# A hybrid decoder trunk on one NeuronCore: half of the modulation rows multiplied on GpSimd and summed by ScalarE, with three tiles for them and four for raw weights

## The chip, the cores and the metric

The kernel runs on one NeuronCore of a Trainium2 chip. The metric is the device time of one execution in microseconds (us). TensorE (PE) multiplies matrices; VectorE (DVE), ScalarE (ACT) and GpSimd (POOL) work element by element; SyncE (SP) issues nearly all transfers from device memory. Each engine works through its own queue in order and waits for others by semaphores.

## The reference, cut to what matters

A trunk of two layers over 256 tokens of 2048 features in float32. Each of its four sub-layers (mixer and FFN of layer 0, mixer and FFN of layer 1) is modulated by shift, scale and gate, which come from one vector `c`:

```python
def ada_modulation(c, w, b):
    mod = (jax.nn.silu(c) @ w + b)[:, None, :]
    shift, scale, gate = jnp.split(mod, 3, axis=-1)
    return shift, scale, gate

def swiglu(h, w1, w3, w2):
    return (jax.nn.silu(h @ w1) * (h @ w3)) @ w2

    for i in range(DEPTH):
        shift, scale, gate = ada_modulation(c, ada_mix_w[i], ada_mix_b[i])
        h = rms_norm(x) * (1.0 + scale) + shift
        ...
        x = x + gate * y
        shift, scale, gate = ada_modulation(c, ada_ffn_w[i], ada_ffn_b[i])
        h = rms_norm(x) * (1.0 + scale) + shift
        x = x + gate * swiglu(h, ffn_w1[i], ffn_w3[i], ffn_w2[i])
    return rms_norm(x) * final_norm_w
```

Each `w` of the modulation is 2048 x 6144, so four of them are 201 MB of the 706 MB that the kernel moves. As `c` is one row, this product is not made on TensorE. The mixer of layer 0 runs RWKV-7 and a gated delta rule side by side, that of layer 1 is Mamba-2.

## The kernel before

**Matrix products.** Activations lie transposed, features on partitions and 256 tokens along the row. A float32 product is made of three TensorE products in a rounded format: weights and activations are split in a high and a low part (`whi`, `wlo`; `hhi`, `hlo`, and so on), and high x high, high x low and low x high are summed in PSUM (`products`, L749). Weights stream in through `raw` tiles of up to 128 x 1024 (512 KB; RAW = 5, L89). ScalarE rounds a tile to `whi`, VectorE subtracts to get `wlo` (`split_next` L659, `low_parts` L703), then the `raw` tile is free for the next load. Of `whi` and `wlo` there are three each (PARTS, L92), so that `whi` is made about two pieces ahead of its use.

**Slabs.** The first product of a sub-layer runs as a slab (`lin_slab`, L775): 16 rows, one for each 128 features of the normalised input, and in each row several output tiles, so that TensorE can start on feature block 0 while later blocks are still being normalised. In a row VectorE multiplies `t` by the norm, ScalarE adds the shift and rounds to `hhi`, VectorE subtracts to `hlo` (`norm_mod`, L840, `shifted`). The shift of row kt has to be known by then (`modc`, L650). In the first slab of all, that of layer 0's mixer, the norm's multiply (`xin`) and `hlo` run on GpSimd (`first`, L1913).

**Modulation rows.** 128 outputs of a modulation are one row (l, r, n): sub-layer l, r = 0 for shift, 1 for scale, 2 for gate, block n of 16. The shift and scale of the first sub-layer are made from 1 MB tiles (`ini`) in the first slab. The other 160 rows are halved, 128 x 1024 each (512 KB), and loaded into `adat` tiles (ADAS = 2). For each of the 320 halves VectorE multiplies by the broadcast silu(c) (`silc`) and sums in one instruction (`ada_half`, L620; CUSTOM_DVE_ANT_0 in the trace, ISA in the program, followed by a read of the accumulator, DVE_READ_ACCUMULATOR2_ANT). The second half starts from the first's sum, so they go in order; the first starts from the bias. A scale gets 1.0 added.

**What sets the order.** The Python code writes the instructions of all engines in one sequence and holds each engine to it. A clock with estimated costs (`Clock.cost`, L301) runs along. Main thread is TensorE's stream of products; after each step the code lets chains of the mixers go on, makes pieces ahead, and calls `fill_ada` (L633). That places a half on VectorE when by the clock VectorE is 500 ns behind TensorE, or at most 2000 ns ahead if the half is due. Halves queue in `adaq`, spread over the weights of the stages ahead by `plan` (L551), and may be loaded up to 48 weight tiles early (`issue_ada`, L612). Where `modc` needs a row that isn't known yet, it takes halves at once, wherever that stands in VectorE's order. All loads, of `raw` and of `adat`, go through SyncE's queue in the order in which they were written; one that waits for its tile holds those behind it.

Of the kernel before, what the change touches and what calls it, by code (L numbers as in the profile page):

```python
# [10 lines left out]
F32 = mybir.dt.float32  # L11
# [7 lines left out]
P = 128  # L19
# [66 lines left out]
LAG = 4  # L86
SOON = 1000.0
INI = 6
RAW = 5  # L89
PIECE = 8  # L90
LEAD = 2
PARTS = 3  # L92
WORK0 = 6
WORK1 = 10
IDLE = 500.0
ADAS = 2
FILL = -500.0
LATE = 2000.0
DUE = 1.0
# [154 lines left out]
class Clock:  # L254
# [46 lines left out]
    def cost(self, i, name):  # L301
        e = i.engine
        o = i.outs[0]
        n = max(self.n(x) for x in list(i.outs) + list(i.ins) if getattr(x, "ap", None))
        t = mybir.EngineType
        if e == t.PE:
            nn, m = self.n(o), self.n(i.ins[1])
            if name == "transpose":
                return 109.0
            if i.ins[0].dtype == F32R:  # L310
                return max(107.0, 0.425 * nn)
            if m <= 64:
                return max(50.0 if m <= 32 else 81.0, 1.05 * nn)
            return max(430.0 if nn < 60 else 214.0, 1.68 * nn)
        if e == t.DVE:
            ps = any(getattr(getattr(x, "bass_ap", None), "tensor", None) is not None
                     and x.bass_ap.tensor.name.startswith("bank") for x in list(i.outs) + list(i.ins))
            if name in ("tensor_scalar", "tensor_copy") and not ps:
                return 65.0 + 0.53 * n
            return (130.0 if name == "scalar_tensor_tensor" else 70.0) + 1.05 * n  # L320
        if e == t.Activation:
            return 95.0 + 0.83 * n
        if e == t.Pool:
            return 500.0 if n <= 16 else 120.0 + (4.0 if name == "tensor_scalar" else 2.4) * n
        return 60.0

# [69 lines left out]
def trunk(ctx: ExitStack, tc: tile.TileContext, I, out):  # L396
# [180 lines left out]
    ifree = list(range(INI))  # L577
    st = {"raw": 0, "item": 0, "off": 0, "hold": True}
    lows = []
    raws, parts, known, sums = {}, [], set(), {}  # L580
    after_ada = {}
    adat = [wp.tile([P, 1024], F32, name=f"adat{q}") for q in range(ADAS)]
    aname = [name_of(t) for t in adat]
    adas = []

    def load_ada(t, l, r, n, e):
        SP.dma_start(t, I["ada"][l, 16 * r + n, e])
# [22 lines left out]
        issue_raw()  # L610

    def issue_ada():  # L612
        while adaq and len(adas) < ADAS and adaq[0][4] <= st["item"] + EARLY:
            q = next(q for q in range(ADAS) if q not in [a[0] for a in adas])
            if adas and clock.since(aname[q]) > clock.at(ET.PE) + QUEUE:
                return
            adas.append((q,) + adaq.pop(0))
            load_ada(adat[q], *adas[-1][1:5])

    def ada_half(t, l, r, n, e):  # L620

        if e == 0:
            sums[l, r, n] = cp.tile([P, 1], F32, tag="adap", name=nm("adap"), bufs=6)
        pt = sums[l, r, n]
        o = mod[:, l, 16 * r + n:16 * r + n + 1] if e else pt
        V.tensor_tensor_reduce(t, t, silc[:, 1024 * e:1024 * (e + 1)], 1.0,
                               pt if e else prc("adab", 48 * l + 16 * r + n), ALU.mult, ALU.add, o)
        if e:
            if r == 1:
                V.tensor_scalar(o, o, 1.0, None, ALU.add)  # L630
            known.add((l, r, n))

    def fill_ada(until=None):  # L633

        issue_ada()
        while adas:
            q, l, r, n, e, due = adas[0]
            v = clock.at(ET.DVE)
            if until is None:
                until = clock.at(ET.PE) + (LATE if due <= st["item"] else FILL)  # L640
# [4 lines left out]
    def take_ada():  # L645
        q = adas.pop(0)
        ada_half(adat[q[0]], *q[1:5])
        issue_ada()

    def modc(l, r, n):  # L650
        while (l, r, n) not in known:
            if not adas:
                q = adaq[0][:4] + (0,)
                adaq[0] = q
                issue_ada()
            take_ada()
        return mod[:, l, 16 * r + n:16 * r + n + 1]

    def split_next(rows=None):  # L659
# [1320 lines left out]
```

## Time and profile before

| | us |
|---|---|
| median of 3 runs | 3011.66 (3009.58 to 3016.07) |
| the profiled execution's own time | 3014.75 |
| its span, first to last instruction | 3012.9 |
| mean granted TensorE clock | 0.981 |
| waits of VectorE for loads of `adat` | 30.7, in 33 places |

The stages in the profiled execution, in us from the span's start: 30 to 145 the first slab, 145 to 740 the rest of layer 0's mixer and its output product, 744 to 812 the slab of layer 0's FFN, to 1500 the rest of that FFN, 1560 to 2080 the Mamba mixer after its slab, 2290 to 3012 the FFN of layer 1 after its slab. A row of a group gives, after the operands and the count, the busy time in us, the mean of one in ns, the idle time of the engine before it in us, and what ended that idle time. In a timeline the first two numbers are the start and the duration in us; in brackets stands the idle time before it and what ended it. All instructions are recorded by one helper, so that the line (L372) tells nothing and the tiles' names tell all.

### The profile page before, as it was taken

How to read it: one execution, taken by the hardware profiler on the slowest of the kernel's cores; microseconds unless marked ns; L12 is line 12 of the kernel's file. 1: busy time of each engine (PE TensorE's matmuls, PEld its weight loads, DVE VectorE, ACT ScalarE, POOL GpSimd, SP SyncE). 2: the span in 40 equal slices, each digit the busy share in tenths (PEclk: the TensorE clock that was granted, in tenths of full speed). 3: DMA queues.
4: the chain of work that ended last, by engine and by line, in shares of the span. 5: the costliest groups of instructions: out<-in, count | busy, mean ns of one | idle time of the engine just before them, and what ended most of it. 6: DMA issues, size and time to landing. Idle time of an engine off the chain costs nothing.

```text
span 3012.9 us, 61369 instructions
## 1 busy us (share of the span) xinstructions
PE 2884.7 (96%) x25095; PEld 2816.0 (93%) x25095; DVE 2199.6 (73%) x3438; ACT 1440.2 (48%) x2358; POOL 172.5 (6%) x191
## 2 busy tenths in 40 slices
PE   6789999998799999999999999999999999999998
PEld 6788889888699999999999999999999999999998
DVE  6987888888677787677768878888867745554555
ACT  3354546544344444444456556555445444444444
POOL 3400101100000000000000111111000000000000
PEclk9998999999899999999999999999999999999999
DMA  9865565577687898877865666666866755655554
GB/s 396 345 199 176 173 221 162 174 251 260 223 320 278 286 332 308 285 270 261 261 221 200 207 213 229 214 233 218 281 225 236 273 185 174 200 184 191 185 174 153
DMA packets 236730, 706.29 MB, mean 234 GB/s; under 512 B 36848, under 2 KB 55584, under 8 KB 236192
## 3 DMA queue, kind: packets, MB, share of 16 engines
q1 hardware_dynamic: 235872, 699.46, 67.9%
q8 instruction: 196, 3.21, 0.4%
q10 hardware_dynamic: 576, 2.92, 0.2%
q14 instruction: 86, 0.70, 0.1%
HBM read 695.70 MB, written 6.58 MB: 233 GB/s over the span
## 4 chain that ended last, share of the span: by engine, by line
issue 52%; PE 21%; DVE 2%; ACT 1%; DMA 0%; POOL 0%; DVEq 0%; POOLq 0%; ACTq 0%
PE bank L372 21%; DVE wlo L372 1%; ACT whi L372 0%; DMA adat<-in_ada 0%; DVE w L372 0%; DVE ymix L372 0%; DVE x L372 0%; POOL mgsa L372 0%; ACT mar L372 0%; DVE adat L372 0%; DVE mar L372 0%; ACT t L372 0%; DVE mxs L372 0%; DVE hlo L372 0%; DVE t0b L372 0%
## 5 line engine op out<-in xcount | busy, mean ns | idle before, releaser
L372 PE MATMUL bank<-hhi,whi 128*128 128x256 f32 x5568 | 1477.5, 287 | 35.3 <-ACT whi L372 33.9
L372 PE MATMUL bank<-hlo,whi 128*128 128x256 f32 x5568 | 1455.1, 283 | 6.9 <-DVE hlo L372 6.9
L372 DVE TENSOR_TENSOR wlo<-raw,whi 128x1024 fp32r<-128x1024 f32 (+3 forms) x1001 | 1112.5, 1125 | 438.8 <-ACT whi L372 433.6
L372 ACT ACTIVATE whi<-raw 128x1024 fp32r<-128x1024 f32 (+3 forms) x1001 | 967.9, 975 | 683.5 <-PE bank L372 659.5
L372 PE MATMUL bank<-hhi,wlo 128*128 128x256 f32 x5568 | 1126.6, 284 | 31.1 <-DVE wlo L372 30.9
L372 PEld LDWEIGHTS bank<-hhi,whi 128*128 128x128 f32 x5568 | 1064.0, 191 | 53.9 <-ACT whi L372 39.6
L372 PEld LDWEIGHTS bank<-hlo,whi 128*128 128x128 f32 x5568 | 1063.9, 191 | 10.4 <-DVE hlo L372 8.5
L372 PEld LDWEIGHTS bank<-hhi,wlo 128*128 128x128 f32 x5568 | 861.8, 190 | 41.7 <-DVE wlo L372 36.1
L372 PE MATMUL bank<-glo,whi 128*128 128x256 f32 x1408 | 351.1, 281 | 0.0
L372 PE MATMUL bank<-ghi,whi 128*128 128x256 f32 x1408 | 351.0, 281 | 0.0
L372 PEld LDWEIGHTS bank<-glo,whi 128*128 128x128 f32 x1408 | 265.0, 188 | 0.0
L372 PEld LDWEIGHTS bank<-ghi,whi 128*128 128x128 f32 x1408 | 265.0, 188 | 0.0
L372 PE MATMUL bank<-ghi,wlo 128*128 128x256 f32 x1408 | 229.6, 281 | 0.0
L372 DVE CUSTOM_DVE_ANT_0 adat<-adat,silc,adap 128x1024 f32<-128x1024 f32 x160 | 211.7, 1323 | 20.2 <-DMA adat<-in_ada 19.2
L372 DVE CUSTOM_DVE_ANT_0 adat<-adat,silc,prm 128x1024 f32<-128x1024 f32 x160 | 208.5, 1303 | 11.9 <-DMA adat<-in_ada 11.5
L372 PEld LDWEIGHTS bank<-ghi,wlo 128*128 128x128 f32 x1408 | 193.8, 188 | 0.0
L372 ACT ACTIVATE fs<-bank 128x256 f32<-128x256 f32 x88 | 33.9, 385 | 194.7 <-PE bank L372 194.7
L372 DVE TENSOR_TENSOR fg<-fs,bank 128x256 f32<-128x256 f32 x88 | 37.0, 420 | 111.5 <-ACT fs L372 111.5
L372 DVE SCALAR_TENSOR_TENSOR w<-pad,prm,w 128x256 f32<-128x256 f32 x216 | 110.0, 510 | 5.2
L372 POOL TENSOR_TENSOR rstd<-rpow,half_neg 128x2 f32<-128x2 f32 x5 | 3.5, 696 | 1774.2 <-DVE rpow L372 1774.2
L372 DVE CUSTOM_DVE_ANT_0 ini<-ini,silc,prm 128x2048 f32<-128x2048 f32 x32 | 84.7, 2646 | 15.9 <-DMA prm<-in_prm 15.9
L372 DVE SCALAR_TENSOR_TENSOR x<-bank,mod,x 128x256 f32<-128x256 f32 x106 | 50.6, 481 | 48.1 <-PE bank L372 48.0
(253 smaller groups left out, 2043.4 us busy)
## 6 DMA issues: line engine op xcount, KB each, us to landing
raw<-in_ffn SPq DMA_DIRECT2D x352, 512.0 KB, 4.6
adat<-in_ada SPq DMA_DIRECT2D x320, 512.0 KB, 4.8
raw<-in_in SPq DMA_DIRECT2D x238, 512.0 KB, 3.5
raw<-in_ffn SPq DMA_DIRECT2D x128, 384.0 KB, 3.6
raw<-in_ffn SPq DMA_DIRECT2D x128, 320.0 KB, 4.5
raw<-in_out SPq DMA_DIRECT2D x75, 512.0 KB, 4.9
ini<-in_ada SPq DMA_DIRECT2D x32, 1024.0 KB, 8.2
raw<-in_in SPq DMA_DIRECT2D x48, 448.0 KB, 5.2
```

Source lines behind the costliest of these rows:

```text
L372: r = f(*a, **k)
```

## The change

A half that has been loaded may now go to GpSimd and ScalarE: GpSimd multiplies it by `silc` in four pieces of 256 columns, in place (`ada_slow`), and one ScalarE instruction copies the tile onto itself and sums it by its accumulator (`sum_slow`). At most two halves are in work so, and a piece is placed when by the clock GpSimd is at most 1000 ns ahead of TensorE. The sum is placed on ScalarE when by the clock the last piece was done 700 ns ago. VectorE still takes halves as before, where the queue has any left. As the two halves of a row may come from different engines, their sums lie apart, and a small VectorE instruction adds them, with bias and 1.0 (`ada_end`). There are three `adat` tiles and four `raw` tiles in place of two and five, and the clock counts a GpSimd multiply at 6 ns a column.

```diff
--- before.py
+++ after.py
@@ -86,14 +86,17 @@
 LAG = 4
 SOON = 1000.0
 INI = 6
-RAW = 5
+RAW = 4
 PIECE = 8
 LEAD = 2
 PARTS = 3
 WORK0 = 6
 WORK1 = 10
 IDLE = 500.0
-ADAS = 2
+ADAS = 3
+GAHEAD = 1000.0
+GPIECE = 256
+GSLACK = 700.0
 FILL = -500.0
 LATE = 2000.0
 DUE = 1.0
@@ -321,6 +324,9 @@
         if e == t.Activation:
             return 95.0 + 0.83 * n
         if e == t.Pool:
+            if name == "tensor_tensor" and n > 64:
+
+                return 120.0 + 6.0 * n
             return 500.0 if n <= 16 else 120.0 + (4.0 if name == "tensor_scalar" else 2.4) * n
         return 60.0
 
@@ -577,11 +583,13 @@
     ifree = list(range(INI))
     st = {"raw": 0, "item": 0, "off": 0, "hold": True}
     lows = []
-    raws, parts, known, sums = {}, [], set(), {}
+    raws, parts, known = {}, [], set()
+
+    slow, rec, ends = [], {}, []
     after_ada = {}
     adat = [wp.tile([P, 1024], F32, name=f"adat{q}") for q in range(ADAS)]
     aname = [name_of(t) for t in adat]
-    adas = []
+    adas, held = [], set()
 
     def load_ada(t, l, r, n, e):
         SP.dma_start(t, I["ada"][l, 16 * r + n, e])
@@ -610,31 +618,92 @@
         issue_raw()
 
     def issue_ada():
-        while adaq and len(adas) < ADAS and adaq[0][4] <= st["item"] + EARLY:
-            q = next(q for q in range(ADAS) if q not in [a[0] for a in adas])
+        while adaq and len(held) < ADAS and adaq[0][4] <= st["item"] + EARLY:
+            q = min((q for q in range(ADAS) if q not in held), key=lambda q: clock.since(aname[q]))
             if adas and clock.since(aname[q]) > clock.at(ET.PE) + QUEUE:
                 return
             adas.append((q,) + adaq.pop(0))
+            held.add(q)
             load_ada(adat[q], *adas[-1][1:5])
 
+    def sum_of():
+        return cp.tile([P, 1], F32, tag="adap", name=nm("adap"), bufs=8)
+
+    def ada_end(key):
+
+        l, r, n = key
+        sums, biased, _ = rec[key]
+        if not biased:
+            sums = sums + [prc("adab", 48 * l + 16 * r + n)]
+        if r == 1:
+            sums = sums + [1.0]
+        o = mod[:, l, 16 * r + n:16 * r + n + 1]
+        if len(sums) > 1:
+            V.tensor_scalar(o, sums[0], sums[1], sums[2] if len(sums) > 2 else None, ALU.add,
+                            *([ALU.add] if len(sums) > 2 else []))
+            if len(sums) > 3:
+                V.tensor_scalar(o, o, sums[3], None, ALU.add)
+        known.add(key)
+
+    def ada_done(key):
+        rec[key][2] += 1
+        if rec[key][2] == 2:
+            ends.append((key, max(clock.since(name_of(a)) for a in rec[key][0])))
+
     def ada_half(t, l, r, n, e):
 
-        if e == 0:
-            sums[l, r, n] = cp.tile([P, 1], F32, tag="adap", name=nm("adap"), bufs=6)
-        pt = sums[l, r, n]
-        o = mod[:, l, 16 * r + n:16 * r + n + 1] if e else pt
-        V.tensor_tensor_reduce(t, t, silc[:, 1024 * e:1024 * (e + 1)], 1.0,
-                               pt if e else prc("adab", 48 * l + 16 * r + n), ALU.mult, ALU.add, o)
-        if e:
-            if r == 1:
-                V.tensor_scalar(o, o, 1.0, None, ALU.add)
-            known.add((l, r, n))
+        key = (l, r, n)
+        q = rec.setdefault(key, [[], False, 0])
+        if q[0]:
+            first = q[0].pop()
+        else:
+            first, q[1] = prc("adab", 48 * l + 16 * r + n), True
+        o = mod[:, l, 16 * r + n:16 * r + n + 1] if q[2] else sum_of()
+        V.tensor_tensor_reduce(t, t, silc[:, 1024 * e:1024 * (e + 1)], 1.0, first, ALU.mult, ALU.add, o)
+        q[0].append(o)
+        ada_done(key)
+
+    def ada_slow():
+
+        if slow and slow[0][2] == 1024:
+            q, key, o, e = slow[0]
+            if clock.since(aname[q]) + GSLACK < clock.at(ET.Activation):
+                sum_slow()
+        for z in slow:
+            q, key, o, e = z
+            if o < 1024:
+                if clock.at(ET.Pool) <= clock.at(ET.PE) + GAHEAD:
+                    G.tensor_tensor(adat[q][:, o:o + GPIECE], adat[q][:, o:o + GPIECE],
+                                    silc[:, 1024 * e + o:1024 * e + o + GPIECE], ALU.mult)
+                    z[2] += GPIECE
+                return
+
+    def sum_slow():
+        q, key, o, e = slow.pop(0)
+        for o in range(o, 1024, GPIECE):
+            G.tensor_tensor(adat[q][:, o:o + GPIECE], adat[q][:, o:o + GPIECE],
+                            silc[:, 1024 * e + o:1024 * e + o + GPIECE], ALU.mult)
+        a = sum_of()
+        S.activation(adat[q], adat[q], AF.Copy, accum_out=a)
+        rec[key][0].append(a)
+        held.discard(q)
+        ada_done(key)
+        issue_ada()
 
     def fill_ada(until=None):
 
         issue_ada()
+        ada_slow()
+        while ends and ends[0][1] + GSLACK < clock.at(ET.DVE):
+            ada_end(ends.pop(0)[0])
         while adas:
             q, l, r, n, e, due = adas[0]
+            if len(slow) < 2 and clock.since(aname[q]) < clock.at(ET.PE) and clock.at(ET.Pool) <= clock.at(ET.PE) + GAHEAD:
+                adas.pop(0)
+                rec.setdefault((l, r, n), [[], False, 0])
+                slow.append([q, (l, r, n), 0, e])
+                ada_slow()
+                continue
             v = clock.at(ET.DVE)
             if until is None:
                 until = clock.at(ET.PE) + (LATE if due <= st["item"] else FILL)
@@ -645,15 +714,26 @@
     def take_ada():
         q = adas.pop(0)
         ada_half(adat[q[0]], *q[1:5])
+        held.discard(q[0])
         issue_ada()
 
     def modc(l, r, n):
-        while (l, r, n) not in known:
-            if not adas:
-                q = adaq[0][:4] + (0,)
-                adaq[0] = q
-                issue_ada()
-            take_ada()
+        key = (l, r, n)
+        while key not in known:
+            for i, q in enumerate(ends):
+                if q[0] == key:
+                    ends.pop(i)
+                    ada_end(key)
+                    break
+            else:
+                if any(z[1] == key for z in slow) or (not adas and slow):
+                    sum_slow()
+                    continue
+                if not adas:
+                    q = adaq[0][:4] + (0,)
+                    adaq[0] = q
+                    issue_ada()
+                take_ada()
         return mod[:, l, 16 * r + n:16 * r + n + 1]
 
     def split_next(rows=None):
```

Of the 320 halves, 237 go to GpSimd and ScalarE (948 multiplies, 237 sums), 83 stay on VectorE.

The first place is GpSimd's queue in the first slab: `xin` is the norm's multiply three rows ahead, `hlo` the low part of the row's input. Before:

```order
L372 TENSOR_TENSOR rstd_183<-rpow_184,half_neg 128x2
L372 TENSOR_TENSOR xin<-xin,rb_189 128x256 x4
L372 TENSOR_TENSOR hlo<-tin,hhi 128x256
L372 TENSOR_TENSOR xin<-xin,rb_189 128x256
L372 TENSOR_TENSOR hlo<-tin,hhi 128x256
```

And now, from the fifth row of the slab on:

```order
L378 TENSOR_TENSOR hlo<-tin,hhi 128x256
L378 TENSOR_TENSOR adat_112<-adat_112,silc 128x256 x2
L378 TENSOR_TENSOR xin<-xin,rb_189 128x256
L378 TENSOR_TENSOR hlo<-tin,hhi 128x256
L378 TENSOR_TENSOR adat_112<-adat_112,silc 128x256 x2
L378 TENSOR_TENSOR adat_113<-adat_113,silc 128x256
L378 TENSOR_TENSOR xin<-xin,rb_189 128x256
```

Pieces of halves, 25 in all up to the last `hlo`, now stand between `hlo` and `xin`; before, the two alternated.

The second place is VectorE's queue in the slab of layer 0's FFN: `t` is the normalised row, `bank` holds the norm's factor, `adap` a partial sum, and the row of `mod` is a known shift. Before:

```order
L372 TENSOR_TENSOR t_7682<-t_7682,bank_74 128x256
L372 ISA adat_113,adap_8419<-adat_113,silc,prm 128x1024
L372 ISA adap_8419 128x1
L372 ISA adat_114,mod<-adat_114,silc,adap_8419 128x1024
L372 ISA mod 128x1
L372 SCALAR_TENSOR_TENSOR hlo<-t_7682,mod,hhi 128x256
L372 TENSOR_TENSOR wlo_8426<-raw_99,whi_8425 128x1024
```

And now:

```order
L378 TENSOR_TENSOR t_8036<-t_8036,bank_76 128x256
L378 SCALAR_TENSOR_TENSOR hlo<-t_8036,mod,hhi 128x256
L378 TENSOR_TENSOR wlo_8712<-raw_99,whi_8711 128x1024
L378 TENSOR_TENSOR t_8036<-t_8036,bank_76 128x256
L378 SCALAR_TENSOR_TENSOR hlo<-t_8036,mod,hhi 128x256
L378 TENSOR_TENSOR wlo_8748<-raw_100,whi_8747 128x1024
L378 TENSOR_SCALAR mod<-adap_8647,adap_8717,prm 128x1
```

The halves between `t` and `hlo` (14 in this slab) are gone from VectorE; the 96 halves that the slab needs stand ahead of it. What stays is the add of two partial sums, of a row that is needed later.

The third place is ScalarE's queue in the up-projection of layer 0's FFN; `fs` is the silu of a product, `ghi` the high part of the FFN's inner activation. Before:

```order
L372 ACTIVATE whi_12845<-raw_99 128x1024
L372 ACTIVATE fs_12873<-bank_76 128x256
L372 ACTIVATE ghi_8672<-fg_12874 128x256
L372 ACTIVATE whi_12890<-raw_100 128x1024
L372 ACTIVATE whi_12909<-raw_101 128x1024
L372 ACTIVATE whi_12939<-raw_102 128x1024
```

And now:

```order
L378 ACTIVATE fs_13644<-bank_72 128x256
L378 ACTIVATE ghi_9067<-fg_13645 128x256
L378 ACTIVATE adat_114,adap_13652<-adat_114 128x1024
L378 ACTIVATE whi_13666<-raw_102 128x1024
L378 ACTIVATE adat_113,adap_13669<-adat_113 128x1024
L378 ACTIVATE whi_13696<-raw_99 128x1024
```

Sums of halves, each of which waits for GpSimd, now stand in ScalarE's queue ahead of the weights' high parts.

## The prediction

> **What bounds the kernel now.** I read the page's totals first, then the windows by stage (busy us of each engine, in brackets its instructions; then granted TensorE clock, DMA share, GB/s).
>
> ```profile
> PE 2884.7 (96%) x25095; PEld 2816.0 (93%) x25095; DVE 2199.6 (73%) x3438; ACT 1440.2 (48%) x2358; POOL 172.5 (6%) x191
> core 0: us, PE busy (x) PEld busy (x) DVE busy (x) ACT busy (x) POOL busy (x), PEclk, DMA share, GB/s
> 30.00:145.00 115.00, 89.14 (x626) 85.10 (x626) 108.01 (x102) 45.21 (x65) 56.51 (x41) 0.93 0.94 373
> 145.00:740.00 595.00, 557.01 (x5690) 514.24 (x5689) 496.02 (x1126) 308.82 (x699) 46.17 (x88) 0.95 0.62 204
> 744.00:812.00 68.00, 48.56 (x330) 45.81 (x330) 44.36 (x74) 22.15 (x32) 0.69 (x1) 0.88 0.53 183
> 2249.00:2290.00 41.00, 39.98 (x325) 39.29 (x324) 26.32 (x45) 21.11 (x31) 0.69 (x1) 0.96 0.46 160
> 870.00:1500.00 630.00, 630.00 (x5327) 630.00 (x5326) 468.98 (x639) 275.84 (x355) 0.00 (x0) 1.00 0.83 287
> 1560.00:2080.00 520.00, 516.11 (x4418) 501.93 (x4416) 434.36 (x657) 313.88 (x563) 59.68 (x44) 1.00 0.64 219
> ```
>
> TensorE is the bound, and it idles in few places: 26 us of the first slab (30 to 145), where VectorE is busy 94% of the time; 38 us over the rest of layer 0; 19 us of the slab of layer 0's FFN (744 to 812). In the bulk of that FFN (870 to 1500) it is busy throughout and in the Mamba mixer (1560 to 2080) for 99%; there a lighter VectorE can win next to nothing. So I weigh the first slab, the FFN slab and the rest of layer 0, and ask of the two long stages only what they could lose.
>
> **The FFN slab: what goes.** The two rows 744:812 and 2249:2290 are the same work, a slab of 16 rows with eight units each, in the FFNs of layers 0 and 1. VectorE's timeline gives their first and last instructions; the groups below are those of 744 to 812.
>
> ```profile
> 744.04 0.16 DVE L372 TENSOR_SCALAR rpow<-bank 128x2 f32<-128x2 f32 x1 [1.21 <-PE bank L372]
> 811.23 0.48 DVE L372 SCALAR_TENSOR_TENSOR hlo<-t,mod,hhi 128x256 fp32r<-128x256 f32 x1
> 2249.40 0.16 DVE L372 TENSOR_SCALAR rpow<-bank 128x2 f32<-128x2 f32 x1 [0.75 <-PE bank L372]
> 2289.85 0.48 DVE L372 SCALAR_TENSOR_TENSOR hlo<-t,mod,hhi 128x256 fp32r<-128x256 f32 x1
> L372 DVE CUSTOM_DVE_ANT_0 adat<-adat,silc,adap 128x1024 f32<-128x1024 f32 x7 | 9.0, 1283 | 6.8 <-DMA adat<-in_ada 6.8
> L372 DVE CUSTOM_DVE_ANT_0 adat<-adat,silc,prm 128x1024 f32<-128x1024 f32 x7 | 9.0, 1280 | 0.8 <-DMA adat<-in_ada 0.8
> L372 DVE DVE_READ_ACCUMULATOR2_ANT adap<- 128x1 f32 x7 | 0.6, 83 | 0.0
> ```
>
> From `rpow` to the last `hlo` it is 67.2 us in layer 0 and 40.4 in layer 1, 26.7 us more (the lower granted clock, 0.88 against 0.96, is inside this). The difference is the 14 forced halves: 14 x (1.28 + 0.08) = 19.0 us of work and 7.6 us of waits for their loads, together 26.6. A shift must be known before its row's `hhi`, and the queue of halves is behind. In the changed order all 96 halves that this slab needs are finished ahead of it, and no `adat` stands between its `hlo` on VectorE. So 26.7 us go; next late is TensorE itself, as in layer 1.
>
> **What it adds: a piece's price.** 237 of 320 halves become four GpSimd multiplies each, with one ScalarE sum. The first slab already has GpSimd multiplies of this size beside VectorE (both timelines):
>
> ```profile
> 34.27 0.74 POOL L372 TENSOR_TENSOR xin<-xin,rb 128x256 f32<-128x256 f32 x1
> 45.28 2.78 POOL L372 TENSOR_TENSOR xin<-xin,rb 128x256 f32<-128x256 f32 x1
> ```
> ```profile
> 40.36 2.34 DVE L372 CUSTOM_DVE_ANT_0 ini<-ini,silc,prm 128x2048 f32<-128x2048 f32 x1
> 42.62 2.09 DVE L372 TENSOR_TENSOR wlo<-raw,whi 128x896 fp32r<-128x896 f32 x2
> 44.63 2.83 DVE L372 CUSTOM_DVE_ANT_0 ini<-ini,silc,prm 128x2048 f32<-128x2048 f32 x1
> 47.58 2.63 DVE L372 CUSTOM_DVE_ANT_0 ini<-ini,silc,prm 128x2048 f32<-128x2048 f32 x1
> 52.15 2.82 DVE L372 CUSTOM_DVE_ANT_0 ini<-ini,silc,prm 128x2048 f32<-128x2048 f32 x1
> L372 DVE CUSTOM_DVE_ANT_0 ini<-ini,silc,prm 128x2048 f32<-128x2048 f32 x28 | 75.3, 2689 | 0.0
> ```
>
> Alone, a multiply of 256 columns takes 0.74 us. At 45.28 it takes 2.78: it ends only after VectorE's multiply of 44.63 has. And VectorE pays too: its multiply takes 2.34 us undisturbed, 2.83 after GpSimd's `hlo` and 2.63 after its `xin`, so 0.49 and 0.29 more, **0.39 us a piece**. The mixer shows the same with larger pieces:
>
> ```profile
> 1642.32 2.50 POOL L372 TENSOR_TENSOR mce<-mce,mbc 128x1024 f32<-128x1024 f32 x1 [6.56 <-ACT mce L372]
> ```
> ```profile
> 1642.80 3.10 DVE L372 CUSTOM_DVE_ANT_0 adat<-adat,silc,adap 128x1024 f32<-128x1024 f32 x1
> ```
>
> A half of 1.28 us took 3.10 beside 1024 columns: 1.82 more, 0.46 for each 256. So a half on GpSimd takes up to 4 x 0.39 = 1.56 us from VectorE where VectorE only reads SBUF twice, against 1.36 saved. The Trainium skill, SBUF — State Buffer, section "SBUF: two separate sides", has a rule that speaks against the change: a VectorE instruction with two SBUF inputs and a GpSimd one that reads SBUF share a port pair, and the later one is blocked for the other's whole instruction. The rows agree; it is the ground of the first rival.
>
> **First slab.** VectorE is dense, a row takes 7.51 us (44.63 to 52.15). The new order puts 25 pieces between its `hlo` multiplies and 11 more before its last weights. 36 x 0.39 = 14 us, less one half that leaves VectorE (1.4): **+12 us**. Bounds: 25 x 0.29 = +7, and 36 x 0.74 = +27 if each piece stops VectorE for its whole length. Nine loads instead of three are 3 MB, 8 us at 373 GB/s; the share of 0.94 leaves 7 us, the longer slab the rest, so I count nothing.
>
> **FFN slab, net.** 26 pieces now lie beside its 16 rows. Two rows of layer 1's slab on VectorE:
>
> ```profile
> 2255.78 1.22 DVE L372 TENSOR_TENSOR wlo<-raw,whi 128x1024 fp32r<-128x1024 f32 x1 [1.13 <-ACT whi L372]
> 2257.25 0.48 DVE L372 SCALAR_TENSOR_TENSOR hlo<-t,mod,hhi 128x256 fp32r<-128x256 f32 x1
> 2258.86 1.22 DVE L372 TENSOR_TENSOR wlo<-raw,whi 128x1024 fp32r<-128x1024 f32 x1 [1.13 <-ACT whi L372]
> ```
>
> Of a row's 3.08 us, `wlo` (1.22) and `hlo` (0.48) read SBUF twice, a share of 0.55: 26 x 0.39 x 0.55 = 6. So **-21 us**; bounds -27 (no delay) and -7 (0.74 each).
>
> **Rest of layer 0.** The halves there (windows, by tile), the waits of TensorE from 200 to 700 (us, times, longest), two groups of small steps:
>
> ```profile
> 145.00:744.00 599.00, 104.48 (x82) 0.95 0.62 205
> PE bank L372 <- DVE hlo L372: 6.6, 3, 3.2
> PE bank L372 <- DVE wlo L372: 4.9, 5, 2.3
> PE bank L372 <- ACT whi L372: 4.5, 3, 2.7
> L372 DVE TENSOR_SCALAR mod<-mod 128x1 f32<-128x1 f32 x14 | 2.1, 153 | 0.5
> L372 POOL TENSOR_TENSOR sm<-rpow,half_neg 128x2 f32<-128x2 f32 (+1 forms) x24 | 26.0, 1084 | 234.3 <-DVE rpow L372 234.1
> ```
>
> 82 halves are on VectorE there; of the new order 33 stay, and 232 pieces come. Saved: 49 x 1.36 = 67 us, less some 35 more adds of partial sums at 0.15, 5 us. Added: between 0 and 232 x 0.39 = 90, since much of this stage reads PSUM; I take half, 45, near the share of 0.55 above. So 17 of VectorE's 496 us go, and it gets delays of half a us where it had 1.3 us in one piece. Of the 16 us of waits above I take a third off: **-5 us**. Bounds: -25, with all these waits and the low clock after them gone, and +18: on GpSimd the 24 small steps of the mixer's chains now queue behind pieces, and if each waits for one and TensorE for each, it is 24 x 0.74.
>
> **The long stages.** ScalarE's sum reads 1024 columns, as the widest `whi` does:
>
> ```profile
> L372 ACT ACTIVATE whi<-raw 128x1024 fp32r<-128x1024 f32 x142 | 150.5, 1060 | 125.2 <-PE bank L372 123.4
> ```
>
> 237 x 1.06 = 251 us more on ScalarE; what the accumulator adds no row shows, so 1.06 to 1.5 us each, and I take the lower, the row's. Its cover is the 123 us in which `whi` waits for TensorE in that FFN, where 90 sums (95 us) come. Behind a sum that waits for GpSimd stands the next `whi`, made two pieces ahead of TensorE; were that cover gone, each sum would cost up to 1 us. Behind the final add on VectorE, which waits for the sum, stands `wlo`, with the same lead.
>
> Four raw tiles: a load (SyncE's row) has the time until its tile's `whi`.
>
> ```profile
> 1060.49 0.33 SPq L372 DMA_DIRECT2D raw<-in_ffn  x1
> ```
> ```profile
> 1066.35 0.85 ACT L372 ACTIVATE whi<-raw 128x768 fp32r<-128x768 f32 x1 [1.04 <-PE bank L372]
> 1068.49 0.74 ACT L372 ACTIVATE whi<-raw 128x640 fp32r<-128x640 f32 x1 [1.29 <-PE bank L372]
> raw<-in_ffn SPq DMA_DIRECT2D x128, 320.0 KB, 4.5
> ```
>
> With five tiles that is the fifth `whi` (1068.49), 8.0 us on; with four the fourth (1066.35), 5.9 us, and landing takes 4.5. It holds by 1.4 us, and by 2.1 more (the distance of the two `whi`) through their lead. On SyncE's queue a half's load now waits for ScalarE's sum instead of VectorE's multiply, and raw loads stand behind it; such waits were 2.3 us each from 690 to 900:
>
> ```profile
> SPq L372 <- DVE adap L372: 39.8, 17, 5.7
> ```
>
> That is within 1.4 + 2.1, but only just. I take **+3 us** for both stages, bounds 0 and +20.
>
> **Sum.** 12 - 21 - 5 + 3 = -11 us. Against the profiled execution's 3014.75 us (span 3012.9 and 1.9 around it) that is 3003.8; it lies 3.1 above the median shown, 3011.66, so **3001 us**.
>
> **Rivals.**
> - **The port takes it back (slower).** If each piece holds VectorE near its full 0.74, the first slab gains 27 us instead of 12, the FFN slab keeps only -7, layer 0 turns to +5: +27 - 7 + 5 + 3 = +28, 3040 us. For it: four VectorE instructions a row leave GpSimd four turns, and 4.5 of its instructions now stand in a row. Against it: the measured 0.29 to 0.49. In the two slabs 62 pieces meet 27 us, so with the other terms it turns at about 0.45 us a piece. By the skill's rule, whole instructions, it would be this case.
> - **Given back (no change).** The forced halves go, but the first slab costs 18 us (0.49 a piece) and layer 0 gains nothing: -21 + 18 + 3 = 0, 3012 us. For it: the port's time is nearly conserved (1.56 against 1.36 a half).
> - **More relief.** Pieces mostly meet PSUM reads: 7 - 27 - 16 + 0 = -36, 2976 us, with all 16 us of layer 0's waits gone. Against it: dense rows.
> - **Late weights.** With four tiles a load that lands after 7.9 us stalls TensorE; 64 short loads by 0.5 us are +32 - 11, 3033 us. Against it: 4.5 us to landing.
>
> **How the numbers follow.** My forecast 0.38, port 0.26, given back 0.21, more relief 0.11, late weights 0.04. A run tells 0.2%, 6 us, from no change. Faster: 0.38 + 0.11, less 0.02 where the forecast falls inside 6 us: 0.47. Same: 0.21 + 0.02 = 0.23. Slower: 0.30. The range takes in relief and port, 2974 to 3040. The forecast alone: 2990 to 3006.
>
> **What would show it.** The FFN slab's `rpow` to last `hlo` falls from 67 to about 46 us, with no `adat` on VectorE. The first slab's rows grow from 7.5 to 8.3 us, `ini` near 2.8 on average over the 2.69 now. `wlo` of 1024 columns exceeds 1.22 in 870 to 1500, with TensorE still at 100%. ScalarE near 1690 us, VectorE within 60 us of 2200. It is wrong if the slab still waits, if rows pass 9 us, or if TensorE idles for `whi` after loads.

## The result, and the profile after

The changed kernel takes **3111.01 us** (median of 4 runs, 3106.44 to 3113.90), the kernel before 3010.62 beside it: a ratio of 1.0329, 95% interval 1.0310 to 1.0348. It is slower by 100 us, and lies far outside the predicted range. Medians here and below are of all runs; in five sets of runs one run took 16% longer or more, which moves no median by more than 0.8 us. The totals of the profiled execution (span 3108.5 us):

```profile
PE 2942.3 (95%) x25095; PEld 2859.7 (92%) x25095; DVE 2143.5 (69%) x3093; ACT 1670.5 (54%) x2832; POOL 1166.1 (38%) x1139
```

VectorE is 56 us lighter and ScalarE 230 us heavier, both near the forecast. TensorE's busy time, which no edit touched, is 58 us longer. To see where, I cut both executions at the same work. Of the 1001 `whi` in ScalarE's timeline, the starts of numbers 1, 34, 151, 201, 476, 701 and 1001 are the borders; the lengths between them are in us, and the last four columns are experiments of the next section (`a_` is built on the changed kernel, `b_` on the one before; the three `a_` columns have the changed kernel's tiles).

| stage | before | after | a_onein | a_tiny | a_tiny2 | b_tiles |
|---|---|---|---|---|---|---|
| first slab | 115.1 | 128.8 | 122.6 | 119.4 | 120.0 | 115.2 |
| rest of layer 0's mixer | 533.7 | 575.2 | 539.2 | 528.1 | 518.6 | 532.1 |
| to the end of the FFN slab | 190.1 | 175.0 | 166.7 | 165.8 | 162.9 | 175.0 |
| rest of layer 0's FFN | 675.6 | 688.1 | 684.8 | 683.2 | 685.1 | 674.6 |
| Mamba mixer to the FFN slab of layer 1 | 709.8 | 740.5 | 730.2 | 730.6 | 723.9 | 707.7 |
| rest of layer 1's FFN | 736.6 | 749.0 | 747.7 | 747.6 | 746.8 | 736.6 |

Only the stage with the FFN slab gained. Its first and last instructions on VectorE now:

```profile
806.84 0.16 DVE L378 TENSOR_SCALAR rpow<-bank 128x2 f32<-128x2 f32 x1 [1.21 <-PE bank L378]
853.07 0.78 DVE L378 SCALAR_TENSOR_TENSOR hlo<-t,mod,hhi 128x256 fp32r<-128x256 f32 x1
```

From `rpow` to the last `hlo` it is 46.2 us instead of 67.2, with no half between them. Now windows over the other stages, first before, then after (columns as in the prediction):

```profile
149.00:682.00 533.00, 503.70 (x5283) 462.42 (x5282) 441.38 (x1032) 277.30 (x648) 44.10 (x86) 0.96 0.60 195
1562.00:2070.00 508.00, 504.19 (x4324) 490.84 (x4323) 423.86 (x645) 306.50 (x555) 59.68 (x44) 1.00 0.64 219
2650.00:2850.00 200.00, 200.00 (x1707) 200.00 (x1707) 100.69 (x108) 88.66 (x107) 0.00 (x0) 1.00 0.58 187
```
```profile
162.00:737.00 575.00, 520.07 (x5279) 472.86 (x5278) 458.52 (x970) 331.22 (x755) 236.55 (x306) 0.94 0.57 188
1616.00:2153.00 537.00, 517.68 (x4314) 500.47 (x4313) 426.28 (x603) 341.99 (x627) 228.31 (x210) 0.99 0.62 216
2745.00:2945.00 200.00, 200.00 (x1669) 200.00 (x1668) 97.69 (x103) 85.95 (x104) 0.00 (x0) 1.00 0.56 185
```

Three things show. In the rest of layer 0's mixer VectorE has 62 instructions less and is busy 17 us *more*; TensorE's idle time grows from 29 to 55 us there, and its granted clock falls from 0.96 to 0.94. The Mamba mixer's idle time grows from 4 to 19 us. And in the last row, in layer 1's FFN, where GpSimd is idle, no half is left and TensorE never waits, 200 us hold 1669 matmuls instead of 1707: **119.8 ns each instead of 117.2**, at a clock of 1.00 in both. Nothing in the prediction could make that.

The first slab, GpSimd and then VectorE, in two fences of timeline rows:

```profile
60.22 5.52 POOL L378 TENSOR_TENSOR adat<-adat,silc 128x256 f32<-128x256 f32 x2
65.70 1.58 POOL L378 TENSOR_TENSOR xin<-xin,rb 128x256 f32<-128x256 f32 x1
67.24 1.59 POOL L378 TENSOR_TENSOR hlo<-tin,hhi 128x256 fp32r<-128x256 f32 x1
68.79 7.06 POOL L378 TENSOR_TENSOR adat<-adat,silc 128x256 f32<-128x256 f32 x3
```
```profile
59.58 2.83 DVE L378 CUSTOM_DVE_ANT_0 ini<-ini,silc,prm 128x2048 f32<-128x2048 f32 x1
62.52 2.63 DVE L378 CUSTOM_DVE_ANT_0 ini<-ini,silc,prm 128x2048 f32<-128x2048 f32 x1
65.09 3.14 DVE L378 TENSOR_TENSOR wlo<-raw,whi 128x896 fp32r<-128x896 f32 x2
68.15 2.83 DVE L378 CUSTOM_DVE_ANT_0 ini<-ini,silc,prm 128x2048 f32<-128x2048 f32 x1
```

The two engines go in step: each GpSimd instruction ends some 0.6 us after one of VectorE's, so that it takes 2.76 us beside an `ini` and 1.58 beside a `wlo`; and the two `wlo` take 3.14 where they took 2.09. Over the slab, `wlo` before and then `wlo` and `ini` after:

```profile
L372 DVE TENSOR_TENSOR wlo<-raw,whi 128x896 fp32r<-128x896 f32 x32 | 34.7, 1123 | 8.3 <-ACT whi L372 8.3
L378 DVE TENSOR_TENSOR wlo<-raw,whi 128x896 fp32r<-128x896 f32 x32 | 46.1, 1474 | 9.7 <-ACT whi L378 9.7
L378 DVE CUSTOM_DVE_ANT_0 ini<-ini,silc,prm 128x2048 f32<-128x2048 f32 x28 | 75.7, 2702 | 0.0
```

The delay falls on `wlo`, 11 us in all; `ini` stays at the 2.69 us that it had. A row of four long VectorE instructions costs 8.57 us instead of 7.51 (59.58 to 68.15), and where more than four GpSimd instructions stand in a row, GpSimd sets its length. TensorE's waits over the whole span say so:

```profile
PE bank L378 <- DVE wlo L378: 42.8, 39, 4.3
PE bank L378 <- ACT whi L378: 29.1, 25, 4.8
PE bank L378 <- POOL hlo L378: 13.6, 6, 4.8
```

How a delay reaches TensorE in the mixer, in rows of VectorE, of GpSimd and of TensorE:

```profile
473.35 1.77 DVE L378 TENSOR_TENSOR wlo<-raw,whi 128x1024 fp32r<-128x1024 f32 x1
475.05 2.72 DVE L378 SCALAR_TENSOR_TENSOR w<-pad,prm,w 128x256 f32<-128x256 f32 x3
...
478.65 1.48 DVE L378 SCALAR_TENSOR_TENSOR w<-pad,prm,w 128x256 f32<-128x256 f32 x3
...
481.38 1.23 DVE L378 TENSOR_TENSOR wlo<-raw,whi 128x1024 fp32r<-128x1024 f32 x1
```
```profile
473.29 4.18 POOL L378 TENSOR_TENSOR adat<-adat,silc 128x256 f32<-128x256 f32 x4 [1.42 <-DMA adat<-in_ada]
```
```profile
482.65 0.58 PE L378 MATMUL bank<-hhi,wlo 128*128 128x256 f32 x1 [4.34 <-DVE wlo L378]
```

Four pieces lie from 473.3 to 477.5. Beside them `wlo` takes 1.77 us instead of 1.23 and three `w` take 2.72 instead of 1.48. The next `wlo` stands behind them in VectorE's queue, and TensorE has waited 4.34 us for it, of which these two rows explain 1.8.

### The profile page after: what moved, and what is told of

Read it like the earlier page. It is cut to its first block, busy times and chain, and to the rows that moved or that the text cites. A ratio compares the mean times of both kernels' runs of the same rounds, so it can differ in the third digit from the quotient of the medians.

```text
span 3108.5 us, 62702 instructions
## 1 busy us (share of the span) xinstructions
PE 2942.3 (95%) x25095; PEld 2859.7 (92%) x25095; DVE 2143.5 (69%) x3093; ACT 1670.5 (54%) x2832; POOL 1166.1 (38%) x1139
## 4 chain that ended last, share of the span: by engine, by line
PE 39%; issue 23%; DVE 3%; ACT 3%; DMA 3%; POOL 1%; DVEq 0%; SPq 0%; POOLq 0%; ACTq 0%
PE bank L378 39%; ACT whi L378 1%; DVE wlo L378 1%; DMA adat<-in_ada 1%; DMA raw<-in_ffn 1%; ACT mar L378 1%; DVE w L378 1%; POOL adat L378 1%; ACT adat L378 0%; DVE t0b L378 0%; DVE x L378 0%; DVE t L378 0%; DMA raw<-in_out 0%; DVE adat L378 0%; POOL mxw L378 0%
## 5 line engine op out<-in xcount | busy, mean ns | idle before, releaser
L378 DVE TENSOR_TENSOR wlo<-raw,whi 128x1024 fp32r<-128x1024 f32 (+3 forms) x1001 | 1224.7, 1238 | 568.0 <-ACT whi L378 561.9
L378 PE MATMUL bank<-hhi,whi 128*128 128x256 f32 x5568 | 1496.3, 290 | 34.8 <-ACT whi L378 29.1
L378 PE MATMUL bank<-hlo,whi 128*128 128x256 f32 x5568 | 1470.4, 284 | 20.4 <-POOL hlo L378 13.6
L378 POOL TENSOR_TENSOR adat<-adat,silc 128x256 f32<-128x256 f32 x948 | 994.2, 1078 | 905.2 <-DMA adat<-in_ada 895.5
L378 ACT ACTIVATE whi<-raw 128x1024 fp32r<-128x1024 f32 (+3 forms) x1001 | 957.4, 971 | 582.6 <-PE bank L378 455.0
L378 PE MATMUL bank<-hhi,wlo 128*128 128x256 f32 x5568 | 1138.5, 286 | 41.1 <-DVE wlo L378 41.0
L378 ACT ACTIVATE adat<-adat 128x1024 f32<-128x1024 f32 x237 | 248.3, 1048 | 11.3 <-POOL adat L378 11.2
L378 DVE SCALAR_TENSOR_TENSOR w<-pad,prm,w 128x256 f32<-128x256 f32 x216 | 133.9, 621 | 5.1
L378 DVE CUSTOM_DVE_ANT_0 adat<-adat,silc,prm 128x1024 f32<-128x1024 f32 x75 | 107.9, 1440 | 33.2 <-DMA adat<-in_ada 30.9
```

What stands on the lines that cost most here:

```text
L378: r = f(*a, **k)
```

## The experiments

Two theories at first. **Place**: the matmuls are slower because the weights lie elsewhere. The change adds two partial sums to the small tiles, which lie ahead of `raw`, `adat`, `whi` and `wlo`; each takes 32 bytes of a partition, so all behind them moved by 64 bytes. **Port**: the GpSimd pieces slow VectorE. Rivals: the new waits and order, and four `raw` tiles.

**Place.** `a_realign` is the changed kernel with every engine's order kept, `b_pad64` the kernel before with 64 bytes put in:

```diff
-        return cp.tile([P, 1], F32, tag="adap", name=nm("adap"), bufs=8)
+        return cp.tile([P, 1], F32, tag="adap", name=nm("adap"), bufs=6)
```
```diff
     mod = cp.tile([P, 4, 48], F32, name="mod")
+    cp.tile([P, 16], F32, name="gap")
```

> The changed kernel with six partial sums (adap) in place of eight. The order of every engine is that of the changed kernel; all tiles from raw on lie 64 bytes lower, where they lie before the change (whi at byte 94720 instead of 94784 of a partition). Theory 'place': the matmuls are slower because of where the weights lie; the pitch of the matmuls in the up-projection of layer 1's FFN goes from 120.0 ns back to 117.3, and with 25095 matmuls that lost about 1.4 ns each on average the time falls by about 35 us, to 3076. Rival 'port only' (GpSimd's pieces alone cost the time): 3111, the pitch stays at 120.0.

> The kernel before with an unused tile of 64 bytes ahead of the raw tiles; nothing else differs, every tile from raw on lies where the changed kernel has it. Theory 'place': pitch of 120.0 ns in the FFN's up-projections, 3011 + 35 = 3046 us. Rival 'port only': 3011, 117.3 ns.

Measured: `a_realign` 3085.67 us, 25 less (ratio to the kernel before 1.0236, 1.0198 to 1.0274); `b_pad64` 3038.17 against 3013.89 beside it, 24 more (ratio 1.0072, 1.0045 to 1.0099). The windows of 200 us in layer 1's FFN, `a_realign` and then `b_pad64`:

```profile
2720.00:2920.00 200.00, 200.00 (x1707) 200.00 (x1706) 100.61 (x107) 87.95 (x108) 0.00 (x0) 1.00 0.59 187
```
```profile
2670.00:2870.00 200.00, 200.00 (x1669) 200.00 (x1668) 98.90 (x104) 86.03 (x105) 0.00 (x0) 1.00 0.57 182
```

The matmul's time follows the place, 1707 and 1669, whichever kernel it is. I had expected 35 us from the mean of the pitches; it is 25. These windows lie in the up-projection, where `hhi` and `hlo` are multiplied. In the down-projection of the same FFN it is `ghi` and `glo`, before and then after:

```profile
2510.00:2610.00 100.00, 100.00 (x845) 100.00 (x845) 50.45 (x65) 40.51 (x51) 0.00 (x0) 1.00 0.60 186
2600.00:2700.00 100.00, 100.00 (x845) 100.00 (x845) 50.42 (x65) 40.41 (x51) 0.00 (x0) 1.00 0.61 185
```

There a matmul takes 118.3 ns in both, though `whi` and `wlo` are the same moved tiles. So the weights' place alone doesn't set the time. Which tiles? `b_padw` puts the 64 bytes behind `adat`:

```diff
     adat = [wp.tile([P, 1024], F32, name=f"adat{q}") for q in range(ADAS)]
+    wp.tile([P, 16], F32, name="gap")
```

> The kernel before with an unused tile of 64 bytes between the adat tiles and whi: raw and adat lie where they do before the change, whi, wlo and all behind them 64 bytes higher. Theory 'place of what TensorE reads': the whole loss of b_pad64, 3011 + 25 = 3036. Rival 'place of what the transfers write' (raw, adat): 3011.

Measured: 3039.30 us (ratio 1.0090, 1.0074 to 1.0106). The whole loss is there with `raw` and `adat` at their old place: what counts is where the tiles from `whi` on lie. Why 64 bytes count, and why only for `hhi` and `hlo`, stays open.

**Pieces.** `a_tiny` keeps the order, since the clock still counts 256 columns, and leaves GpSimd next to nothing to do; `a_onein` keeps the length and takes one input away (for it too the clock counts a piece as before; `...` stands for lines left out):

```diff
         if e == t.Pool:
+            if name == "tensor_tensor" and o.bass_ap.tensor.name.startswith("adat"):
+                n = GPIECE
...
-                    G.tensor_tensor(adat[q][:, o:o + GPIECE], adat[q][:, o:o + GPIECE],
-                                    silc[:, 1024 * e + o:1024 * e + o + GPIECE], ALU.mult)
+                    G.tensor_tensor(adat[q][:, o:o + 8], adat[q][:, o:o + 8],
+                                    silc[:, 1024 * e + o:1024 * e + o + 8], ALU.mult)
...
```
```diff
...
-                    G.tensor_tensor(adat[q][:, o:o + GPIECE], adat[q][:, o:o + GPIECE],
-                                    silc[:, 1024 * e + o:1024 * e + o + GPIECE], ALU.mult)
+                    G.tensor_scalar(adat[q][:, o:o + GPIECE], adat[q][:, o:o + GPIECE], 1.0, None, ALU.mult)
...
```

> The changed kernel with the same order on every engine, but each GpSimd piece multiplies 8 columns instead of 256 (most of the products of 237 halves are left out, so the modulation is not computed). Theory 'port': the pieces' load on SBUF is what slows VectorE and queues up on GpSimd; the first slab returns to about 115 us, the mixers lose their extra waits, the FFN slab keeps its gain of 15: 3011 - 15 + 35 (if the matmuls stay slow for the place) = 3031, or 2996 without that part. Rival 'waits' (the sums on ScalarE, the additions and the new order cost it, whatever a piece lasts): above 3090.

> The changed kernel, same order, but each GpSimd piece multiplies its 256 columns by the constant 1.0: one input from SBUF instead of two (the product with silu(c) is left out for 237 halves). Theory 'two inputs lock': an instruction of GpSimd with a single input runs beside VectorE without a mutual stop, wlo of 1024 columns is back at 1.22 us, and the time is near that of a_tiny, 3033 to 3050. Rival 'any GpSimd work on SBUF': VectorE is as slow as in the changed kernel, 3100 or more.

Measured: `a_tiny` 3032.61 us (ratio to the kernel before 1.0057, 1.0039 to 1.0075), `a_onein` 3046.03 (1.0096, 1.0067 to 1.0126). Groups of the changed kernel, of `a_onein`, and of the kernel before:

```profile
L378 POOL TENSOR_TENSOR adat<-adat,silc 128x256 f32<-128x256 f32 x948 | 994.2, 1078 | 905.2 <-DMA adat<-in_ada 895.5 <-PE bank L378 5.5 <-ACT whi L378 2.5
L378 DVE TENSOR_TENSOR wlo<-raw,whi 128x1024 fp32r<-128x1024 f32 x665 | 890.0, 1351 | 408.5 <-ACT whi L378 402.8 <-PE bank L378 2.4 <-DMA scrA<-nAT 1.4
```
```profile
L380 POOL TENSOR_SCALAR adat<-adat 128x256 f32<-128x256 f32 x948 | 1029.7, 1109 | 842.3 <-DMA adat<-in_ada 834.4 <-PE bank L380 6.4
L380 DVE TENSOR_TENSOR wlo<-raw,whi 128x1024 fp32r<-128x1024 f32 x665 | 828.3, 1256 | 461.8 <-ACT whi L380 457.9 <-DMA scrA<-nAT 1.8 <-DMA raw<-in_in 1.2
```
```profile
L372 DVE TENSOR_TENSOR wlo<-raw,whi 128x1024 fp32r<-128x1024 f32 x665 | 808.9, 1230 | 298.5 <-ACT whi L372 293.7 <-PE bank L372 2.1 <-DMA raw<-in_in 1.1
```

GpSimd is as busy with one input as with two, but `wlo` is nearly back at its old mean, and 65 us of time go. So GpSimd's work as such is not what makes VectorE slow. The two instructions differ in the second input and, with it, in the operation (TENSOR_SCALAR for TENSOR_TENSOR); I take it to be the input. The Trainium skill, SBUF — State Buffer, section "Who interferes with whom", lets a VectorE instruction with two SBUF inputs contend with any GpSimd instruction that reads SBUF; here VectorE hardly noticed one that reads a single operand (1.256 us instead of 1.230), and the measurement decides. The mixer's windows, `a_onein`, `a_tiny` and `b_pad64`:

```profile
157.00:696.00 539.00, 505.82 (x5279) 463.42 (x5279) 409.04 (x970) 330.90 (x755) 247.37 (x298) 0.97 0.62 200
```
```profile
153.00:681.00 528.00, 499.92 (x5280) 458.18 (x5279) 393.55 (x970) 330.89 (x755) 97.65 (x293) 0.98 0.64 204
151.00:681.00 530.00, 498.05 (x5287) 456.92 (x5287) 440.84 (x1031) 277.18 (x650) 43.26 (x86) 0.98 0.62 196
```

In the kernels with the change the same 970 VectorE instructions take 393.6 us with tiny pieces, 409.0 with one input and 458.5 with two, and the stage 528, 539 and 575. With 212 pieces there, a whole piece costs VectorE (458.5 - 393.6) / 212 = 0.31 us. Over the whole kernel it is (2143.5 - 1930.8) / 948 = 0.22, with 1930.8 from the totals of `a_tiny`.

**Sums.** ScalarE's sums read 8 columns instead of 1024, with tiny pieces (`a_tiny2`) and with whole ones (`a_tinysum`); the clock counts them as before:

```diff
...
-        S.activation(adat[q], adat[q], AF.Copy, accum_out=a)
+        S.activation(adat[q][:, :8], adat[q][:, :8], AF.Copy, accum_out=a)
```

> As a_tiny (pieces of 8 columns, the order that of the changed kernel), and ScalarE's sums read 8 columns instead of 1024 too; the products and the sums of 237 halves are left out. a_tiny is 3033, and 21 us of it go in the Mamba mixer, where pieces hardly load anything. Theory 'sums': ScalarE's 251 us of sums delay whi there, and the time falls by about 13 more (17 less the part of the place) to 3020. Rival 'order': the new order of the chains costs it, and the time stays at 3033.

> The changed kernel with its whole GpSimd pieces, but ScalarE's sums read 8 columns instead of 1024 (the sums of 237 halves are left out). Between a_tiny and a_tiny2 the same edit was worth 28 us. Theory 'sums add up with the rest': 3111 - 28 = 3083. Rival 'sums matter only where nothing else is late': with the pieces' delays on VectorE the whi have time, and less than 10 us go, 3101 or more.

Measured: 3005.06 us (ratio 0.9974, 0.9958 to 0.9990), 28 less than `a_tiny`, where I expected 13; and 3076.77 (ratio 1.0215, 1.0201 to 1.0230), 34 less than the changed kernel. The sums cost about 30 us, and they add up with the pieces. The sums' two groups in the changed kernel:

```profile
L378 ACT ACTIVATE adat<-adat 128x1024 f32<-128x1024 f32 x237 | 248.3, 1048 | 11.3 <-POOL adat L378 11.2
L378 ACT ACTIVATION_READ_ACCUMULATOR adat<-adat 128x1 f32 x237 | 44.7, 189 | 0.0
```

They wait only 11 us for GpSimd; what they cost is 1.24 us each in ScalarE's queue. In the profiled `a_tinysum`, 20 us of the gain are in layer 0's mixer (554.8 for 575.2) and 9 in the Mamba stage (732.0 for 740.5); TensorE's waits for `whi` in the former are 3.0 us for 7.3. That mixer in `a_tinysum`:

```profile
163.00:718.00 555.00, 508.95 (x5282) 464.86 (x5281) 457.96 (x970) 287.25 (x756) 230.36 (x304) 0.96 0.61 194
```

TensorE idles 46 us there instead of 55, and is busy 11 us less at a clock of 0.96 instead of 0.94; whether the clock follows from the shorter idle time no run shows. Some 8 us of the Mamba stage stay even in `a_tiny2` over `b_pad64` (715.9); I put that down to the new order, untested.

**Tiles.** The kernel before with the changed numbers of tiles alone, twice:

```diff
-RAW = 5
+RAW = 4
...
-ADAS = 2
+ADAS = 3
```

> The kernel before with four raw tiles and three adat tiles, every half still on VectorE, all other tiles at their old place. Theories 'place' and 'port': four raw tiles are enough, within 8 us of 3011. Rival 'late weights': loads come late, 3033 or more, and TensorE waits for whi after a load.

> The kernel of b_tiles once more, on the chip of a_ffn: four raw and three adat tiles, every half on VectorE. Expected where it was, a ratio of 0.993 to the kernel before, 2996 us.

Neither theory had this. Measured: **2996.30 us**, ratio 0.9933 (0.9909 to 0.9957), and 2998.06, ratio 0.9954 (0.9941 to 0.9967). This part alone beats both kernels. The stage with the FFN slab falls from 190.1 to 175.0 us. The slab's first and last instructions on VectorE in `b_tiles`:

```profile
748.41 0.16 DVE L372 TENSOR_SCALAR rpow<-bank 128x2 f32<-128x2 f32 x1 [1.21 <-PE bank L372]
801.50 0.48 DVE L372 SCALAR_TENSOR_TENSOR hlo<-t,mod,hhi 128x256 fp32r<-128x256 f32 x1
```

That is 53.1 us instead of 67.2: 9 instead of 14 halves are forced, and none of them waits for its load (7.6 us before). So 14 of the 21 us that the changed kernel gained in the slab come with the numbers of tiles alone. ScalarE now waits 36 us for `raw` loads, where it waited for none, but TensorE's waits for `whi` fall from 33.9 to 21.5. The two numbers were not tried apart. `b_early`, on top of it, forces none, and `b_early_h` moves `hhi` and `hlo` besides:

```diff
-LATE = 2000.0
-DUE = 1.0
+LATE = 3000.0
+DUE = 0.9
```
```diff
+    hhi = cp.tile([P, KT, T], F32R, name="hhi")
+    hlo = cp.tile([P, KT, T], F32R, name="hlo")
     cst = cp.tile([P, NCST], F32, name="cst")
...
-    hhi = cp.tile([P, KT, T], F32R, name="hhi")
-    hlo = cp.tile([P, KT, T], F32R, name="hlo")
```

> The kernel before with four raw and three adat tiles as in b_tiles (2996), and halves due after 0.9 of a stage's weights instead of 1.0, placed when VectorE is up to 3000 ns ahead instead of 2000; all halves on VectorE. No half is left between t and hlo in the slab of layer 0's FFN (9 were in b_tiles, 14 before). Theory: the forced halves and their loads were the slab's loss, so 9 x 1.36 = 12 us less than b_tiles, less what the earlier halves cost the mixer: 2984 to 2996. Rival: VectorE is the bound of the mixer, and each half that moves there costs its 1.36 us: 2996 or more.

> As b_early, and hhi and hlo, which every product of the slabs and mixers reads, lie at the start of the partition (byte 16512, a multiple of 128) instead of at 31136 (a multiple of 32 only). If the place of the moving operand matters as that of the weights does, the pitch of 117.3 ns changes by a nanosecond or more and the time by 10 to 30 us, either way; if only the weights' place matters, the time of b_early within 6.

Measured: `b_early` 3018.42 (ratio 1.0019, 1.0003 to 1.0034). The FFN slab's stage gains 8 us more (166.7), but the mixer takes 552.7 instead of 532.1. Its windows, `b_tiles` and then `b_early`:

```profile
150.00:682.00 532.00, 503.36 (x5298) 462.14 (x5298) 450.56 (x1049) 277.24 (x650) 39.10 (x86) 0.96 0.63 203
```
```profile
150.00:702.00 552.00, 507.21 (x5246) 463.19 (x5245) 468.41 (x1074) 273.26 (x635) 42.05 (x86) 0.95 0.63 211
```

18 us more on VectorE, 20 us more of stage: the rival held. In these two the mixer can take about 450 us of VectorE, not 470. The Mamba stage is 12 us longer too (719.4), with one half more; why is open. `b_early_h` is at 3031.88 (ratio 1.0056, 1.0032 to 1.0080), 13 us more than `b_early`. Windows in layer 1's up-projection, `b_early` and then `b_early_h`:

```profile
2660.00:2860.00 200.00, 200.00 (x1707) 200.00 (x1706) 100.57 (x106) 86.74 (x105) 0.00 (x0) 1.00 0.58 187
2665.00:2865.00 200.00, 200.00 (x1688) 200.00 (x1687) 99.97 (x106) 86.74 (x105) 0.00 (x0) 1.00 0.57 184
```

A matmul takes 118.5 ns instead of 117.2. So the place of `hhi` and `hlo` counts too; the direction was not foreseen.

**Where pieces are free.** `a_ffn` is the changed kernel, tiles at their old place (six partial sums), with GpSimd used in layer 0's FFN alone:

```diff
+    ffn_a = len(seq) + 16
     plan(pieces("ffn0"), ada_of(1, (2,)) + ada_of(2, (1, 0, 2)))
+    ffn_b = len(seq)
...
-            if len(slow) < 2 and clock.since(aname[q]) < clock.at(ET.PE) and clock.at(ET.Pool) <= clock.at(ET.PE) + GAHEAD:
+            if ffn_a <= st["item"] < ffn_b and len(slow) < 2 and clock.since(aname[q]) < clock.at(ET.PE) and clock.at(ET.Pool) <= clock.at(ET.PE) + GAHEAD:
```

> The changed kernel with halves given to GpSimd only in layer 0's FFN behind its slab (89 of 237 halves, 356 pieces), where TensorE has no waits and VectorE is busy 74 percent; elsewhere every half is on VectorE; six partial sums, so that the tiles lie as before the change. Theory 'the pieces cost only where VectorE's next result is waited for': as b_tiles with at most 8 us more in that FFN, 2990 to 3004. Rival 'pieces cost wherever they are': 356 of 948 pieces, a share of 0.38 of the 65 + 13 us that the pieces cost, 30 us more than b_tiles, 3026.

Measured: 3006.94 us (ratio 0.9974, 0.9964 to 0.9983), 9 more than `b_tiles5` on the same chip and 3 above the range. That FFN, `a_ffn` and `b_tiles5`:

```profile
852.00:1488.00 636.00, 634.19 (x5364) 633.58 (x5363) 438.32 (x523) 349.59 (x513) 341.82 (x312) 1.00 0.83 283
```
```profile
858.00:1492.00 634.00, 634.00 (x5369) 634.00 (x5367) 469.02 (x636) 276.56 (x358) 0.00 (x0) 1.00 0.83 283
```

312 GpSimd instructions cost 2 us of this stage, where TensorE hardly waits: there the first theory's mechanism holds. Where the other 7 us of the medians lie stays open. The spans of the profiled executions are only 1.4 us apart: cut at the borders of the table, `a_ffn` is 8 us shorter in layer 0's mixer, at a clock of 0.98 instead of 0.96, and 6 us longer in the Mamba stage (715.1 instead of 708.8), where it has no piece. Nothing is gained there either, as VectorE was not late.

**The account.** Each step is a kernel of its own, medians in us: the changed kernel 3111.0, tiles at their old place -25.3 (`a_realign`, with `b_pad64` as its counterpart), then, with the tiles where the change has them, one input instead of two -65.0 (`a_onein`), tiny pieces -13.4 (`a_tiny`), tiny sums -27.6 (`a_tiny2`). All four leave 2980, 31 below the kernel before: 15 to 18 of that are the numbers of tiles (`b_tiles`, `b_tiles5`), the rest I take to be what VectorE's relief is worth once nothing is paid for it. This takes the steps to add up, which was tried for the place (25 and 24) and for the sums (34 with whole pieces, 28 with tiny ones); they were not all measured on one chip, and the kernel before differed by 3 us between them.

## Why the prediction was wrong

- **FFN slab, -21**: right for the slab itself, 46.2 us where about 46 were foreseen. But 14 of the 21 us come with the numbers of tiles alone (`b_tiles`), and the stage around it gained only 15: what lies ahead of the slab's `rpow` in it took 69.4 us instead of 61.7.
- **First slab, +12**: right in size, 13.7, in part by luck. VectorE got 11 us more of work, about what was foreseen, but on `wlo` (up to 0.5 us each), while `ini`, from which the price was taken, stayed as it was. And TensorE also waits 13.6 us for GpSimd's `hlo`, for in this slab GpSimd gets one turn per long VectorE instruction. I had this only as an argument for the rival. My own mark against myself, rows past 9 us, was met in GpSimd's rows: from 67 to 136 us its `hlo` start 8.5 to 11.3 us apart. VectorE's rows take 8.4 to 8.8 us, with one of 9.1.
- **Rest of layer 0, -5, bounds -25 to +18**: wrong, +41.5 in the mixer, and the largest error. Behind "17 of VectorE's 496 us go" stood a saving of 62 us and an added delay of 45. Most of the saving came: 48 us, from 441.4 to 393.6 with tiny pieces, in a window that leaves out the last 60 us of the stage. The step that failed is the added delay. I took 0.19 us a piece for a stage that "reads PSUM" much, and it was 0.31, 65 us in all, so that 17 us came instead of going. The second error was to call delays of half a us milder than a half's 1.3 us, and to take a third off TensorE's waits for it: its idle time grew by 26 us, and at the lower clock it was busy 16 us longer. The planner puts a half where VectorE has time by its clock; a piece's delay falls on whatever VectorE does then, and the planner counts nothing for it. Two pairs fit this. From `b_pad64`, which has the halves of the kernel before, to `a_tiny` 47 us of VectorE's work go, and the stage gains 2 us (530.0 to 528.1), or 11 with tiny sums too (`a_tiny2`, 518.6). From `a_onein` to the changed kernel VectorE gets 49 us of delays, and the stage loses 36. But `b_early`'s 18 us were planned halves and cost 20, so it may be VectorE's load past some 450 us that counts, however it is placed; no run separates the two.
- **Long stages, +3, bounds 0 to +20**: too small; 12.5 us came in the rest of layer 0's FFN and 30.7 in the Mamba stage. The sums were priced right, 1.05 us with 0.19 to read the accumulator, inside 1.06 to 1.5, but their cover was looked up in the FFN alone. There it held (2 us less in `a_tinysum`), in the mixers it did not (20 and 9), and the sums cost about 30 us in all. "Late weights" did not decide: ScalarE waits 74 us for `raw` loads in the changed kernel, where it waited for none, but TensorE's waits for `whi` are 29.1 us instead of 33.9, and with four tiles and no pieces the time fell.
- **No term at all**: the place of the tiles, 25 us. The diff had it (eight partial sums in place of six), and I read past it.
- **The rivals**: "the port takes it back" had the right mechanism for half or more of the 131 us that the account lists, at a wrong price: 0.74 us a piece and 28 us in all; it was 0.22 a piece on VectorE, and 65 to 78 us of the kernel's time.

## What to carry to other kernels

Work on an engine with spare time is not free: look first at what its instructions do to the neighbour that is nearly full, and price a delay in the stage where it falls, since a planner cannot place what it does not count. Where a change mixes tile counts and a new path, run the parts alone: here the small part was worth 15 us and the rest cost 115, 25 of it by the place. And when tiles move, by 64 bytes even, compare a stage without waits before and after; matmuls per 200 us is enough.

## What the hardware showed that I had not expected

- 64 bytes of place changed a matmul of 256 columns of `hhi` or `hlo` from 117.2 to 119.8 ns at a clock of 1.00, and 25 us of the kernel, with no wait in the trace; with `ghi` and `glo` it stayed at 118.3. Only these places were tried; a better one may exist.
- Counted over the changed kernel's 665 `wlo` of 1024 columns, those that no piece overlapped took 1.23 us on average (372 of them), those that two pieces overlapped 1.57 (154). With single-input pieces it was 1.28 (189). GpSimd, in turn, waits for VectorE in both: a piece took 0.74 us with VectorE idle (98 pieces), and about 1.7 in half of those that met nothing but a `wlo` for more than 0.1 us; with one input it took 0.85 with VectorE idle, and 4.3 at most, beside an `hlo` and three `wlo`.
